# One stacked product for the exponents' row and column terms, and one lane transpose a group, in a hybrid RG-LRU and DeltaNet block

## The chip, the cores and the metric

The kernel runs on one core of one Trainium2 chip. The metric is device time in microseconds (us) of one execution, the median over several. The core has five engines with an instruction queue each: TensorE (PE), which multiplies and whose weight loads are shown apart as PEld; VectorE (DVE); ScalarE (ACT); GpSimd (POOL); and SyncE (SP), which issues the DMAs here.

## What is computed

The reference is a two-layer block over 256 latent and 256 context tokens of width 1024. Layer 0 mixes tokens with a bidirectional RG-LRU, layer 1 with a bidirectional gated DeltaNet of 8 query/key heads and 16 value heads of 128; each layer is followed by a SwiGLU feed-forward. The change lies in the DeltaNet:

```python
def step(s, xs):
    qc, kc, vc, gc, bc = xs
    gc = jnp.cumsum(gc, axis=-1)
    diff = gc[..., :, None] - gc[..., None, :]
    decay = jnp.where(incl, jnp.exp(jnp.where(incl, diff, 0.0)), 0.0)
    kb = kc * bc[..., None]
    m = jnp.where(strict, jnp.einsum('bhid,bhjd->bhij', kb, kc) * decay, 0.0)
    rhs = jnp.concatenate([vc * bc[..., None], kb * jnp.exp(gc)[..., None]], axis=-1)
    sol = lax.linalg.triangular_solve(m, rhs, left_side=True, lower=True, unit_diagonal=True)
    ...
    attn = jnp.where(incl, jnp.einsum('bhid,bhjd->bhij', qc, kc) * decay, 0.0)
    o = (jnp.einsum('bhcd,bhde->bhce', qc * jnp.exp(gc)[..., None], s)
         + jnp.einsum('bhij,bhje->bhie', attn, v_new))
    ...
```

`decay` is an exponential of a difference of cumulated gates: a term of the row plus a term of the column, with a mask. The kernel uses chunks of 128 tokens in place of 64: four chunks `c` (two of context, two of latents), two directions `d`, and 16 value heads in four groups `g` of four.

## The kernel before, in words

The program is written with a recorder. Each engine call is noted with its operands, and `flush` (line 391) lists the noted instructions on five engines with estimated costs, in order of readiness and of a priority: the instruction's place in the program plus a bias of its stage (`TUNE["bias"]`, line 75). The lower number goes first; when an instruction can go on two engines (`R.copy`: ACT or DVE; `R.tt`: DVE or POOL) the planner picks one. Tiles with a tag share a ring of `bufs` buffers and get them in the order of the program; a tile waits until an earlier one of its tag has been read for the last time. PSUM banks of the tag `tr` (two) go to whoever asks. The planned order is what is emitted, so every line of the profile is line 612, where `flush` makes the calls, and groups are told apart by the names of tiles.

The DeltaNet layer (profile 640 to 1120 us) is a string of stages, `PROG` (line 73). A(h) makes key, values and query of a head from `dn_w_in` (products into `ps_mm` of three terms, hi and lo parts in fp32r; convolution `cu` on DVE and ACT; transposes `ps_kt`, `ps_vt`), and writes key and values to DRAM. Z(i) makes the output gate's input. For each group g of four value heads:

- E(g), line 1357: the logarithm `lb` of the row's factor minus or plus the cumulated gate `gc`, split into hi and lo parts (`cb`), transposed (`ps_cb`) to `cT` (64 rows); then for each of 8 pairs of chunk and direction a call of `exponents` (line 1275) and one exponential of 128x512 on ACT into `gn`.
- N(g), line 1389: products of the key with itself (`ps_g`), times `gn` in place on DVE; then the 32x32 diagonal blocks of the 32 matrices of `gn` are laid side by side (`lw`, line 1417: four DVE transposes, each of one block of 32 partitions), inverted in a loop of 60 small DVE instructions, and transposed back to `ld`, `ldt`. `lw`, `ld`, `ldt` and L's `lw1`, `lw2` share the tag `lane`, three buffers.
- L(g), line 1432: the rest of the inverse out of blocks of 32 and 64, many small products (`ps_w`, `ps_z`).
- P(g), line 1528: four calls of `exponents` into `ps_a`, eight exponentials of 128x256 into the two tiles `at` (two buffers), times query-key products `ps_kq`.
- C(g), line 1552: the recurrence over the four chunks with `gn`, `at` and key and values read back from DRAM. `gn` has two buffers, so E(g+2) waits for C(g).

W(0) begins the output product (`ps_wo`). A call of `exponents` sums three products of 512 columns in a bank: the column term (64 rows of `cT` as weights, `pick` as the moving side; or, for the second direction in P, 128 rows of `rT` and `npick`), the row term (`own` as weights, `rows` moving, 128 rows) and the mask (`below` and `identr`, 128 rows). `rows`, `own`, `npick` and `pick` are made once, ahead of all groups, lines 1247 to 1274.

Of the kernel before, what the change touches and what calls it, by code (L numbers as in the profile page):

```python
# [42 lines left out]
def _shuffle(sh, pattern, sizes):  # L43
# [18 lines left out]
    for g, n in zip(lhs, sh.shape, strict=True):  # L62
# [3 lines left out]
        for a in g:  # L66
# [554 lines left out]
def hybrid_block(ctx: ExitStack, tc: tile.TileContext, I, out, dbg=None):  # L621
# [625 lines left out]
    id64 = piece(64)  # L1247
    V.tensor_tensor(id64, ident[:, 0:64], ident[:, 64:128], OP.add)
    npick = dn.tile([128, 64], F32R, name="npick")
    V.tensor_scalar(npick, id64, -1.0, None, OP.mult)  # L1250
    pick = dn.tile([128, 32], F32R, name="pick")
    V.tensor_tensor(pick[0:64], ident[0:64, 0:32], ident[0:64, 32:64], OP.add)
    mod4 = piece(4)
    V.tensor_reduce(out=mod4, in_=ident.rearrange("p (m h) -> p h m", h=4), axis=AX.X, op=OP.add)
    own = {}
    for sign in (1, -1):
        own[sign] = dn.tile([128, 16], F32R, name=f"own{sign + 1}")
        t = piece(16)
        V.tensor_reduce(out=t, in_=id64.rearrange("p (i h) -> p i h", h=4), axis=AX.X, op=OP.add)
        V.tensor_scalar(own[sign], t, float(sign), None, OP.mult)  # L1260
    gch = dn.tile([128, 2, 2, 4, 16], F32R, name="gch")
    for d in range(2):
        R.copy(gch[:, d, 0], gc[:, :, d, :])
        V.tensor_tensor(gch[:, d, 1], gc[:, :, d, :], gch[:, d, 0].bitcast(F32), OP.subtract)
    pt = bank("tr", "ps_gt")
    for d in range(2):
        T.transpose(pt[:, 128 * d:128 * d + 128], gch[:, d].rearrange("p a c h -> p (a c h)").bitcast(F32), ident)
    rT = dn.tile([128, 2, 128], F32R, name="rT")
    R.copy(rT, pt[:, 0:256].rearrange("p (d i) -> p d i", d=2))
    rows = []  # L1270
    for d in range(2):
        rows.append(dn.tile([128, 4, 128], F32R, name=f"rows{d}"))
        V.tensor_tensor(rows[d], rT[:, d].bitcast(F32).rearrange("p (o i) -> p o i", o=1).to_broadcast([128, 4, 128]),
                        mod4.rearrange("p (h o) -> p h o", o=1).to_broadcast([128, 4, 128]), OP.mult)
    def exponents(g, c, d, sign, bound, col, to, name="ps_e"):

        ps = bank("tr", name)
        p4 = ps.rearrange("p (h i) -> p h i", h=4)
        i = 4 * c + g
        lhs, rhs, n = col  # L1280
# [76 lines left out]
    def stage_e(g):  # L1357
# [14 lines left out]
        cb = dn.tile([128, 2, 32], F32R, tag="cb", bufs=2, name="cb")  # L1372
        lf = lb.rearrange("p c d h -> p (c d h)")
        V.tensor_copy(cb[:, 0], lf)
        V.tensor_tensor(cb[:, 1], lf, cb[:, 0].bitcast(F32), OP.subtract)
        pt = bank("tr", "ps_cb")
        T.transpose(pt[0:64, 0:128], cb.rearrange("p a s -> p (a s)").bitcast(F32), ident)
        cT = t["cT"] = dn.tile([128, 128], F32R, tag="cT", bufs=2, name="cT")
        V.tensor_copy(cT[0:64], pt[0:64, 0:128])
        for c in range(4):  # L1380
            for d in range(2):
                s = sidx(c, d, 0)
                p4 = exponents(g, c, d, (1, -1)[d], 1, column(t, c, d), [gn])
                S.activation(gn[:, s:s + 4, :], p4, AF.Exp)

    def column(t, c, d):
        return t["cT"][0:64], pick[0:64, 4 * (2 * c + d):4 * (2 * c + d) + 4], 64

    def stage_n(g):
# [444 lines left out]
```

## Time and profile before

| | us |
|---|---|
| median of 3 runs | 1363.38 |
| lowest and highest | 1362.26, 1370.28 |
| profiled execution | 1364.68 |
| its span | 1363.0 |

The profiled execution is the one that the views below come from. Its granted TensorE clock is 0.976 of full speed on the mean. Of the page's groups of instructions, the one that the change removes from DVE reads 16 transposes of 32x1024 with 32.0 us; the exponents' products keep PE busy for 33.9 us in E (`ps_e`, 96 products) and 16.0 us in P (`ps_a`, 48 products). A row of the windows gives for a stretch how long each engine was busy, with the number of instructions, the granted clock and the DMAs' share. Products are pipelined: the duration of one is longer than its distance to the next, so costs are read from starts. In the chain of waits each piece is a start, a length, and the work or wait that held the end back at that time.

### The profile page before, as it was taken

To read this page: it belongs to the slowest core of one execution; us is meant where nothing else is said; L and a number is where in the kernel's file an instruction comes from. 1 tells how busy PE (TensorE), PEld (TensorE's weight loads), DVE (VectorE), ACT (ScalarE), POOL (GpSimd) and SP (SyncE) were. 2 spreads that over 40 slices of the span, in tenths; PEclk is the share of its full clock that TensorE was granted. 3 is DMA by queue.
4 is the path that set the end of the run, shared out by engine and by line. 5 is a ranking of instruction groups with operands and counts; after the bars stand their busy time and mean duration, and the time that the engine had idled before them with its cause. 6 is when DMAs were issued, how large, how long until landed. Compare 5 with 4: busy or idle time off the path is not lost.

```text
span 1363.0 us, 23260 instructions
## 1 busy us (share of the span) xinstructions
PE 1308.6 (96%) x9200; PEld 1110.3 (81%) x9200; DVE 1035.0 (76%) x1851; ACT 564.9 (41%) x1053; POOL 229.6 (17%) x203
## 2 busy tenths in 40 slices
PE   5999999899999999999998999999998998999997
PEld 3677778878888888888867788898798888999997
DVE  5799986988775665557868889798499376877775
ACT  3388773444321111005746656747646431211100
POOL 2000000110100001212524333334243100000000
PEclk9899999899999999999999999999999699999999
DMA  9545423365564665333523222323133025455563
GB/s 352 197 165 188 140 94 114 124 202 196 188 228 164 192 208 183 98 110 125 178 74 129 71 78 79 105 71 121 63 117 117 25 92 180 139 182 180 179 181 116
DMA packets 61261, 195.60 MB, mean 144 GB/s; under 512 B 6752, under 2 KB 9952, under 8 KB 60896
## 3 DMA queue, kind: packets, MB, share of 16 engines
q1 hardware_dynamic: 61152, 194.12, 42.8%
q8 instruction: 72, 1.18, 0.4%
q14 instruction: 37, 0.30, 0.1%
HBM read 184.13 MB, written 9.96 MB: 142 GB/s over the span
## 4 chain that ended last, share of the span: by engine, by line
PE 56%; issue 15%; DVE 6%; ACT 4%; DMA 1%; POOL 0%; POOLq 0%; SPq 0%; ACTq 0%; DVEq 0%
PE ps_mm L612 29%; PE ps_dn L612 9%; PE ps_e L612 2%; PE ps_wo L612 2%; PE ps_y L612 2%; PE ps_w L612 2%; PE ps_z L612 2%; PE ps_s L612 1%; DVE lw L612 1%; PE ps_ks L612 1%; DVE cu L612 1%; PE ps_a L612 1%; PE ps_qs L612 1%; PE ps_o L612 1%; ACT gn L612 1%
## 5 line engine op out<-in xcount | busy, mean ns | idle before, releaser
L612 PE MATMUL ps_mm<-hh,whi 128*128 128x512 f32 (+1 forms) x888 | 327.4, 370 | 8.0 <-DVE cu L612 5.6
L612 PE MATMUL ps_mm<-hl,whi 128*128 128x512 f32 (+1 forms) x888 | 327.3, 370 | 0.9 <-DVE hl L612 0.8
L612 PE MATMUL ps_mm<-hh,wlo 128*128 128x512 f32 (+1 forms) x888 | 326.2, 368 | 1.7 <-POOL wlo L612 1.7
L612 DVE TENSOR_TENSOR wlo<-raw,whi 128x1024 fp32r<-128x1024 f32 (+2 forms) x183 | 220.5, 1205 | 17.4 <-ACT whi L612 8.3
L612 DVE CAST whi<-raw 128x1024 fp32r<-128x1024 f32 (+2 forms) x177 | 120.2, 679 | 145.8 <-PE ps_mm L612 81.0
L612 POOL TENSOR_TENSOR wlo<-raw,whi 128x1024 fp32r<-128x1024 f32 x55 | 132.0, 2402 | 506.5 <-DVE whi L612 351.3
L612 PEld LDWEIGHTS ps_mm<-hh,whi 128*128 128x128 f32 x888 | 169.6, 191 | 40.6 <-issue 9.9
L612 PEld LDWEIGHTS ps_mm<-hh,wlo 128*128 128x128 f32 x888 | 169.7, 191 | 29.6 <-POOL wlo L612 2.4
L612 PEld LDWEIGHTS ps_mm<-hl,whi 128*128 128x128 f32 x888 | 170.0, 192 | 27.4 <-DVE hl L612 2.0
L612 PE MATMUL ps_dn<-fh,wlo 128*128 128x256 f32 (+1 forms) x374 | 122.7, 328 | 0.0
L612 PE MATMUL ps_dn<-fl,whi 128*128 128x256 f32 (+1 forms) x374 | 122.5, 327 | 0.0
L612 PE MATMUL ps_dn<-fh,whi 128*128 128x256 f32 (+1 forms) x374 | 122.2, 327 | 0.0
L612 PE MATMUL ps_mm<-h2h,whi 128*128 128x256 f32 x352 | 100.4, 286 | 1.1 <-ACT h2h L612 1.1
L612 PE MATMUL ps_mm<-h2l,whi 128*128 128x256 f32 x352 | 100.6, 286 | 0.5 <-DVE h2l L612 0.3
L612 PE MATMUL ps_mm<-h2h,wlo 128*128 128x256 f32 x352 | 100.1, 284 | 0.0
L612 ACT ACTIVATE whi<-raw 128x1024 fp32r<-128x1024 f32 (+2 forms) x61 | 63.2, 1036 | 77.8 <-PE ps_mm L612 45.1
L612 ACT ACTIVATE fh<-sg 128x256 fp32r<-128x256 f32 (+1 forms) x43 | 22.4, 522 | 156.4 <-DVE sg L612 156.3
L612 ACT ACT_TABLE_LOAD x59 | 75.7, 1283 | 7.0 <-DMA sm<-small 3.4
L612 PEld LDWEIGHTS ps_dn<-fl,whi 128*128 128x128 f32 x374 | 71.1, 190 | 6.4 <-issue 0.4
L612 PEld LDWEIGHTS ps_dn<-fh,wlo 128*128 128x128 f32 x374 | 71.1, 190 | 6.4 <-issue 0.4
L612 PEld LDWEIGHTS ps_dn<-fh,whi 128*128 128x128 f32 x374 | 71.1, 190 | 6.0
L612 DVE SCALAR_TENSOR_TENSOR x<-ring,cs,x 128x1024 f32<-128x1024 f32 x49 | 63.9, 1304 | 15.4 <-DMA ring<-ada_w 14.4
(326 smaller groups left out, 2544.7 us busy)
## 6 DMA issues: line engine op xcount, KB each, us to landing
ring<-ada_w SPq DMA_DIRECT2D x96, 512.0 KB, 4.5
raw<-ffn_gu SPq DMA_DIRECT2D x88, 512.0 KB, 3.5
raw<-dn_w_in SPq DMA_DIRECT2D x49, 512.0 KB, 3.5
raw<-ffn_down SPq DMA_DIRECT2D x34, 512.0 KB, 3.6
raw<-rg_w_in SPq DMA_DIRECT2D x16, 512.0 KB, 4.5
raw<-ffn_down SPq DMA_DIRECT2D x17, 384.0 KB, 3.4
raw<-dn_w_out SPq DMA_DIRECT2D x12, 512.0 KB, 3.6
raw<-rg_w_out SPq DMA_DIRECT2D x10, 512.0 KB, 3.4
```

The source lines that it names most:

```text
L612: call(*[real(x) for x in args], **{n: real(v) for n, v in kw.items()})
```

## The change

The row term and the column term become one product of 128 rows. Per group, `src` holds the cumulated gate of the group's four heads in hi and lo parts (64 columns), ones (64), `lb` in hi and lo parts (64), ones (64) and the gate's parts again (64). Three transposes of 128 columns each, starting at parts 0, 1 and 3, put these along the partitions in one bank `ps_src`; `spread` multiplies them on DVE, reading PSUM, with masks of 0, 1 and -1 into `X` (4x128 columns, one copy a head), `Y` (8x128, one a pair of chunk and direction, with the sign) and `Y2` (2x128, for P's second direction). `src`, `X`, `Y` and `Y2` have one buffer each and are used by E and P of the group. `exponents` then has two products: weights from `Y` or `Y2` with `X` moving, and the mask as before. The setup's `pick`, `npick`, `own`, `gch`, `rT`, `rows` and its two transposes go; masks `mod4`, `own`, `own2` are made instead.

In N, ACT copies the four rows of diagonal blocks to one tile `lc` of 128x1024 (tag `lane`), and one DVE transpose makes `lw` from it.

The order of stages changes: P0 goes ahead of E1, C0 behind A4 and A5, P1 ahead of E2 and P2 ahead of E3, Z1 ahead of N3. The bias of L0 to L2 goes from -1500 to -2200 (L3 has its own). `g0` in `TUNE` is read nowhere.

```diff
-PROG = "A0 A1 E0 A2 N0 A3 E1 L0 P0 N1 C0 A4 A5 E2 P1 L1 N2 C1 A6 Z0 A7 E3 L2 P2 N3 Z1 C2 Z2 Z3 L3 W0 P3 C3"
+PROG = "A0 A1 E0 A2 N0 A3 P0 E1 L0 N1 A4 A5 C0 P1 E2 L1 N2 C1 A6 Z0 A7 P2 E3 L2 Z1 N3 C2 Z2 Z3 L3 W0 P3 C3"
...
-    def exponents(g, c, d, sign, bound, col, to, name="ps_e"):
+    def spread(out, part, mask, n):
+        V.tensor_tensor(out, part.rearrange("p (o i) -> p o i", o=1).to_broadcast([128, n, 128]),
+                        mask.rearrange("p (n o) -> p n o", o=1).to_broadcast([128, n, 128]), OP.mult)
+    def exponents(lhs, rhs, bound, to, name):
...
-        T.matmul(p4, lhs, rhs.rearrange("p (h o) -> p h o", o=1).to_broadcast([n, 4, 128]), start=True, stop=False, needs=to)
-        T.matmul(p4, own[sign][:, i:i + 1].to_broadcast([128, 128]), rows[d], start=False, stop=False)
+        T.matmul(p4, lhs, rhs, start=True, stop=False, needs=to)
         lhs, rhs = (identr, below) if bound > 0 else (below, identr)
         T.matmul(p4, lhs, rhs.rearrange("p (o i) -> p o i", o=1).to_broadcast([128, 4, 128]), start=False, stop=True)
...
+        src = dn.tile([128, 5, 64], F32R, tag="src", bufs=1, name="src")
+        mine = gc.rearrange("p c d h -> p (c d) h")[:, :, 4 * g:4 * g + 4]
+        hi, lo = (src[:, 0, 32 * i:32 * i + 32].rearrange("p (x h) -> p x h", h=4) for i in range(2))
+        R.copy(hi, mine)
+        V.tensor_tensor(lo, mine, hi.bitcast(F32), OP.subtract)
+        R.copy(src[:, 4], src[:, 0])
+        for i in (1, 3):
+            G.memset(src[:, i].bitcast(F32), 1.0)
...
-        T.transpose(pt[0:64, 0:128], cb.rearrange("p a s -> p (a s)").bitcast(F32), ident)
-        cT = t["cT"] = dn.tile([128, 128], F32R, tag="cT", bufs=2, name="cT")
-        V.tensor_copy(cT[0:64], pt[0:64, 0:128])
...
+        X = t["X"] = dn.tile([128, 4, 128], F32R, tag="ex", bufs=1, name="ex")
+        Y = t["Y"] = dn.tile([128, 8, 128], F32R, tag="ey", bufs=1, name="ey")
+        Y2 = t["Y2"] = dn.tile([128, 2, 128], F32R, tag="ey2", bufs=1, name="ey2")
+        for k, i in enumerate((0, 1, 3)):
+            T.transpose(pt[:, 128 * k:128 * k + 128], src[:, i:i + 2].rearrange("p a x -> p (a x)").bitcast(F32), ident,
+                        needs=[X, Y, Y2])
+        spread(X, pt[:, 0:128], mod4, 4)
+        spread(Y, pt[:, 128:256], own, 8)
+        spread(Y2, pt[:, 256:384], own2, 2)
...
+        lc = dn.tile([128, 32, 32], F32, tag="lane", bufs=3, name="lc")
         w = dn.tile([128, 32, 32], F32, tag="lane", bufs=3, name="lw")
         for b in range(4):
             r = slice(32 * b, 32 * b + 32)
-            V.transpose(w[r], gn[r, :, 32 * b:32 * b + 32].rearrange("p s f -> p f s"))
+            S.activation(lc[r], gn[r, :, 32 * b:32 * b + 32], AF.Copy)
+        V.transpose(w, lc.rearrange("p s f -> p f s"))
...
-                col = (rT[:, 1], npick[:, 16 * (2 + c) + 4 * g:16 * (2 + c) + 4 * g + 4], 128) if d else column(t, 2 + c, 0)
-                p4 = exponents(g, 2 + c, d, 1, (1, -1)[d], col, t["at"], "ps_a")
+                lhs = t["Y2"][:, c] if d else t["Y"][:, 4 + 2 * c]
+                p4 = exponents(lhs, t["X"], (1, -1)[d], t["at"], "ps_a")
```

More of the change, by code (lines that the diff above doesn't have):

```diff
@@ L70, in _shuffle @@
     return a.reshape([int(np.prod([dims[x] for x in g])) for g in rhs])
-PROG = "A0 A1 E0 A2 N0 A3 E1 L0 P0 N1 C0 A4 A5 E2 P1 L1 N2 C1 A6 Z0 A7 E3 L2 P2 N3 Z1 C2 Z2 Z3 L3 W0 P3 C3"
-TUNE = dict(warm=5000, ev=3000, stay=(300, 0), g0=4, early=(1, 2, 4, 6), eb=0, ea=(0, 1, 1, 1), nwo=2, prog=PROG,
-            bias={'C3': -1500, 'N0': 100, 'N': -700, 'Z3': -1200, 'L': -1500, 'E3': 700, 'W': 10000, 'L3': -800, 'E': -300, 'W0': 10000, 'P': -100, 'E0': -300, 'N3': -700, 'P2': 0, 'C': 400, 'A': 700, 'Z': 700, 'C1': 0})
+PROG = "A0 A1 E0 A2 N0 A3 P0 E1 L0 N1 A4 A5 C0 P1 E2 L1 N2 C1 A6 Z0 A7 P2 E3 L2 Z1 N3 C2 Z2 Z3 L3 W0 P3 C3"
+TUNE = dict(warm=5000, ev=3000, stay=(300, 0), early=(1, 2, 4, 6), eb=0, ea=(0, 1, 1, 1), nwo=2, prog=PROG,
+            bias={'C3': -1500, 'N0': 100, 'N': -700, 'Z3': -1200, 'L': -2200, 'E3': 700, 'W': 10000, 'L3': -800, 'E': -300, 'W0': 10000, 'P': -100, 'E0': -300, 'N3': -700, 'P2': 0, 'C': 400, 'A': 700, 'Z': 700, 'C1': 0})
 class _Tile:
@@ L1246, in hybrid_block @@
     R.copy(identr, ident)
[L1247 to L1253, printed above, removed]
-    V.tensor_reduce(out=mod4, in_=ident.rearrange("p (m h) -> p h m", h=4), axis=AX.X, op=OP.add)
[L1255 to L1274, printed above, removed]
-    def exponents(g, c, d, sign, bound, col, to, name="ps_e"):
[L1277 to L1280, printed above, removed]
-        T.matmul(p4, lhs, rhs.rearrange("p (h o) -> p h o", o=1).to_broadcast([n, 4, 128]), start=True, stop=False, needs=to)
-        T.matmul(p4, own[sign][:, i:i + 1].to_broadcast([128, 128]), rows[d], start=False, stop=False)
+    sel = dn.tile([128, 14], F32, name="rowsel")
@@ new lines, in hybrid_block @@
+    mod4, own, own2 = sel[:, 0:4], sel[:, 4:12], sel[:, 12:14]
+    V.tensor_reduce(out=mod4, in_=ident.rearrange("p (m h) -> p h m", h=4), axis=AX.X, op=OP.add)
+    mod32 = piece(32)
+    V.tensor_reduce(out=mod32, in_=ident.rearrange("p (m h) -> p m h", h=4), axis=AX.X, op=OP.add)
+    V.tensor_reduce(out=own, in_=mod32.rearrange("p (x i) -> p i x", i=8), axis=AX.X, op=OP.add)
+    V.tensor_scalar(own[0:64, 1:8:2], own[0:64, 1:8:2], -1.0, None, OP.mult)
+    V.tensor_scalar(own2, own[:, 5:8:2], -1.0, None, OP.mult)
@@ L1283, in exponents @@
+    def spread(out, part, mask, n):
+        V.tensor_tensor(out, part.rearrange("p (o i) -> p o i", o=1).to_broadcast([128, n, 128]),
+                        mask.rearrange("p (n o) -> p n o", o=1).to_broadcast([128, n, 128]), OP.mult)
+    def exponents(lhs, rhs, bound, to, name):
+        p4 = bank("tr", name).rearrange("p (h i) -> p h i", h=4)
+        T.matmul(p4, lhs, rhs, start=True, stop=False, needs=to)
         lhs, rhs = (identr, below) if bound > 0 else (below, identr)
@@ L1371, in stage_e @@
             V.tensor_tensor(lb[:, :, d], lb[:, :, d], gc[:, :, d, 4 * g:4 * g + 4], (OP.subtract, OP.add)[d])
-        cb = dn.tile([128, 2, 32], F32R, tag="cb", bufs=2, name="cb")
-        lf = lb.rearrange("p c d h -> p (c d h)")
-        V.tensor_copy(cb[:, 0], lf)
-        V.tensor_tensor(cb[:, 1], lf, cb[:, 0].bitcast(F32), OP.subtract)
-        pt = bank("tr", "ps_cb")
-        T.transpose(pt[0:64, 0:128], cb.rearrange("p a s -> p (a s)").bitcast(F32), ident)
-        cT = t["cT"] = dn.tile([128, 128], F32R, tag="cT", bufs=2, name="cT")
-        V.tensor_copy(cT[0:64], pt[0:64, 0:128])
+        src = dn.tile([128, 5, 64], F32R, tag="src", bufs=1, name="src")
[6 more added lines that the diff above has]
+            G.memset(src[:, i].bitcast(F32), 1.0)
+        lf = lb.rearrange("p c d h -> p (c d h)")
+        V.tensor_copy(src[:, 2, 0:32], lf)
+        V.tensor_tensor(src[:, 2, 32:64], lf, src[:, 2, 0:32].bitcast(F32), OP.subtract)
+        pt = bank("tr", "ps_src")
+        X = t["X"] = dn.tile([128, 4, 128], F32R, tag="ex", bufs=1, name="ex")
[7 more added lines that the diff above has]
+        spread(Y2, pt[:, 256:384], own2, 2)
         for c in range(4):
@@ L1382, in stage_e @@
                 s = sidx(c, d, 0)
[L1383 to L1387, printed above, removed]
+                S.activation(gn[:, s:s + 4, :], exponents(Y[:, 2 * c + d], X, 1, [gn], "ps_e"), AF.Exp)
     def stage_n(g):
```

## The prediction, made before the changed kernel was run

> **What bounds the kernel now.** I read the page's busy line first, then the table of windows over the DeltaNet stage (640 to 1120 us, the only stage that the change touches), then the list of PE's waits there.
>
> ```profile
> span 1363.0 us, 23260 instructions
> PE 1308.6 (96%) x9200; PEld 1110.3 (81%) x9200; DVE 1035.0 (76%) x1851; ACT 564.9 (41%) x1053; POOL 229.6 (17%) x203
> ...
> 640.00:1120.00 480.00, 461.39 (x4221) 392.49 (x4219) 380.87 (x912) 287.60 (x610) 163.97 (x134) 0.97 0.28 92
> 700.00:720.00 20.00, 15.16 (x76) 12.47 (x77) 19.64 (x29) 7.38 (x10) 7.74 (x4) 0.96 0.26 87
> 1040.00:1080.00 40.00, 35.07 (x544) 31.93 (x543) 19.81 (x39) 20.72 (x39) 9.36 (x8) 0.70 0.20 67
> ...
> PE ps_mm L612 <- DVE cu L612: 5.6, 3, 3.1
> PE ps_wo L612 <- POOL ol L612: 3.2, 2, 2.2
> ```
>
> In a window's row the columns are length, then busy time of PE, PEld, DVE, ACT, POOL, then clock and DMA. PE is busy 461.39 of 480 us, so the stage is TensorE's, with 18.6 us of idle time; DVE is at 381 of 480 and runs full in places (19.64 of 20 at 700 to 720, where PE loses 4.84 us). At 1040 to 1080 the granted clock falls to 0.70. So a product taken off PE should shorten the stage by what it takes there, as long as DVE and the order keep PE fed.
>
> **The exponents' products.** Each of 48 calls of `exponents` (8 in each of four E stages, 4 in each of four P stages) issues three products of 512 columns. The timeline of PE and of its weight loads for one of E's calls, and pieces of the chain of waits (start, length, what):
>
> ```profile
> 682.65 0.48 PE L612 MATMUL ps_e<-pick,cT 64*128 64x512 f32 x1
> 683.06 0.50 PE L612 MATMUL ps_e<-rows,own 128*128 128x512 f32 x1
> 683.40 0.40 PE L612 MATMUL ps_e<-below,identr 128*128 128x512 f32 x1
> 683.73 0.48 PE L612 MATMUL ps_e<-pick,cT 64*128 64x512 f32 x1
> ...
> 682.65 0.18 PEld L612 LDWEIGHTS ps_e<-pick,cT 64*128 64x128 f32 x1 [0.37 <-issue]
> 683.06 0.18 PEld L612 LDWEIGHTS ps_e<-rows,own 128*128 128x128 f32 x1 [0.23 <-issue]
> 683.17 0.19 PEld L612 LDWEIGHTS ps_e<-below,identr 128*128 128x128 f32 x1
> ...
> 348.75 42.19 PE ps_mm L612 x186
> 681.41 1.08 PE ps_e L612 x3
> 982.50 2.13 PE ps_e L612 x6
> 889.13 0.68 PE ps_a L612 x3
> 1032.95 1.07 PE ps_a L612 x3
> 973.37 0.11 PE ps_cb L612
> ```
>
> One call takes 1.08 us from start to start. A dense product of 512 columns takes 42.19/186 = 0.227 us, so three would take 0.68. The other 0.40 stands around the 64-row product: its weights load only when the product before has streamed (PEld idle 0.37), and so do those of the full-height product behind it (0.23), whereas the load of the full-height `below` begins 0.11 us after the full-height `rows` started, under it. E's 32 calls are 17 such pieces of the chain, first and last shown, 32.7 us in all (some are paired by the planner and cost 0.88). P's eight calls with `pick` are at 1.07, its eight with `npick` (128 rows) at 0.68: 14.0 us together.
>
> The change folds column and row terms into one product of 128 rows, so two full-height products stay. At 0.227 each a call is 0.454: E falls to 14.5 (18.2 less), P to 7.3 (6.7 less). Bounds: at best this; at worst the pair costs as `rows` and `below` do now, 0.34 + 0.33 = 0.67, which leaves 11.3 less from E and 3.3 less from P, 14.6 in all. I take the dense value, since the full-height load above is already seen to run under its predecessor. Three transposes a group replace one and the two of the setup go: 12 against 6, at 0.11 each 0.7 us more. PE's net: 24.9 - 0.7 = 24.2 us less.
>
> The Trainium skill speaks against this in "TensorE: Matmul & The Clock Gate", section "The mechanism": weight loads overlap products in flight only when their row groups differ. By that rule the new pair, equal in rows, would wait both times as the 0.67 above, and the sum would hold 14.6 instead of 24.9. The full-height load at 683.17 under the full-height product of 683.06 disagrees with it here.
>
> **The building of X, Y, Y2 and the lane transposes.** Groups of instructions of this stage (count, busy us, mean ns):
>
> ```profile
> L612 DVE STREAM_TRANSPOSE lw<-gn 32x1024 f32<-32x1024 f32 x16 | 32.0, 2001 | 0.3
> L612 DVE STREAM_TRANSPOSE ld<-lw 128x1024 f32<-128x1024 f32 x4 | 8.2, 2050 | 0.1
> L612 DVE TENSOR_TENSOR rows<-rT,scratch 128x512 fp32r<-128x512 f32 x2 | 1.3, 688 | 0.0
> L612 DVE TENSOR_TENSOR wlo<-raw,whi 128x1024 fp32r<-128x1024 f32 (+1 forms) x16 | 17.4, 1088 | 1.8 <-ACT whi L612 1.3
> L612 DVE TENSOR_TENSOR oa<-ps_o,oa 128x256 f32<-128x256 f32 x32 | 13.0, 418 | 0.5 <-PE ps_o L612 0.3
> L612 ACT ACTIVATE whi<-raw 128x1024 fp32r<-128x1024 f32 x30 | 31.7, 1056 | 36.5 <-PE ps_mm L612 21.6 <-issue 11.8 <-POOL wlo L612 2.4
> L612 ACT ACTIVATE gn<-ld 32x512 f32<-32x512 f32 x15 | 9.4, 626 | 0.5 <-DVE ld L612 0.3
> L612 ACT ACTIVATE gn<-ps_e 128x512 f32<-128x512 f32 x32 | 18.6, 596 | 13.9 <-PE ps_e L612 13.7
> L612 ACT ACTIVATE at<-ps_a 128x256 f32<-128x256 f32 x32 | 10.5, 379 | 9.7 <-PE ps_a L612 9.7
> ```
>
> A 32-partition transpose of 1024 columns costs as much as one of 128 partitions (2.00 and 2.05). So a group's four (8.0 us of DVE) become one of 2.05, behind four ACT copies of 32x1024. These aren't in the trace: twice the 0.63 of 32x512 is 1.25, the 128x1024 copy is 1.06; I take 1.06, 4.2 us a group. `spread` makes 512, 1024 and 256 columns: 0.69 + 1.2 + 0.42 = 2.3 us (the middle one between the 1.09 of a row that mixes in narrower ones and twice 0.69). DVE: 16 transposes out and 4 in, 23.8 us less; spreads 9.2 more; the setup's `rows` 1.4 less; the small copies and splits of 32 to 128 columns, some gone and some new, I set against each other: 16 us less net. ACT: 17 us more on 288 of 480 busy, off the path while it stays the lesser engine; without that cover, a group's copies and one transpose are still 6.3 us against 8.0. POOL's added memsets of 64 columns and the removed constants stand beside PE work at 640 to 680 and count nothing; were they bare, each is under 0.7 us (the 512-column `rows` row). No DMA is added or moved to another queue; the stages that load (A, C, Z, W) keep their order among themselves except that C0 follows A4 and A5, so its `kspill` and `vspill` reads on SP's queue come behind those stages' weights. I give that nothing either way: C0 then has more time, not less.
>
> **The stall that goes.** Behind the first group's transposes (DVE and PE, timeline):
>
> ```profile
> 707.64 2.01 DVE L612 STREAM_TRANSPOSE lw<-gn 32x1024 f32<-32x1024 f32 x1
> 711.89 0.36 PE L612 MATMUL ps_mm<-hh,whi 128*128 128x256 f32 x1 [1.70 <-DVE cu L612]
> 715.28 1.93 DVE L612 STREAM_TRANSPOSE lw<-gn 32x1024 f32<-32x1024 f32 x1
> 718.13 0.47 PE L612 MATMUL ps_mm<-hh,whi 128*128 128x512 f32 x1 [3.13 <-DVE cu L612]
> ```
>
> PE waits 1.70 and 3.13 us for convolutions (`cu`) that stand in DVE's queue between four transposes. Six of their eight us leave DVE. Bounds: 0 (another DVE item in their place, or stage P0's masks, which now come first) to 4.8; I take 3. The 3.2 us for `ol` at 1047 are other work and I leave them.
>
> **Waits that are added.** X, Y, Y2 and `src` have one buffer each, so E of a group waits until P of the one before has read them, and P waits for the `at` tiles, which C of the group before that holds. `lane` has three buffers and one tile more passes through.
>
> ```profile
> 792.16 1.99 DVE L612 STREAM_TRANSPOSE lw<-gn 32x1024 f32<-32x1024 f32 x1
> 795.26 0.22 PE L612 MATMUL ps_z<-gn,lw 64*64 64x64 f32 x1
> ...
> 837.30 0.70 PE L612 MATMUL ps_e<-pick,cT 64*128 64x512 f32 x2
> 838.97 1.72 PE L612 MATMUL ps_o<-yy,at 128*128 128x128 f32 x14
> ```
>
> E2 begins at 837.4 now, before C0's last reads of `at` (to 840.7). Then P1 has 8 exponentials of 0.38 (3.0 us), the three transposes 0.33, and X and Y take 1.9 before E2's first product: about 845.9, 8.5 us later than now. Behind that wait on DVE stand `cu` and `r` of other stages, on PE only the products of this group. E2 itself goes at ACT's 0.60 a call, not at 1.02 (3.4 us back), and N2 wins 1.7: 3.4 us late in sum. N1's transpose needs the slot that `ps_z<-gn,lw` of L0 frees at 795.5, so it ends at 797.6, not 794.2: 3.4 late. Both delays have A products beside them, so I price them 0; bare, they are 6.8 us. E0 starts 1.9 later behind X and Y, under A2's products: 0.
>
> **Sum.** 1364.68 (the profiled execution, span 1363.0) - 24.2 - 3 = 1337.5. That execution is 1.3 us above the median of the runs, 1363.38; I say 1337.
>
> **Rivals.** (a) The groups' chain E, N, L, C sets the length, and PE's saved time turns to idle. For it: DVE at 381 of 480 and the single buffers. Against: 18.6 us idle in the whole stage. Then E2's 3.4 and N1's 3.4 are paid, the stall's 3 comes back, E0, E1, E3 are each shorter by 8 times 0.42 less the 1.9 of the masks: near 1364.7 + 6.8 - 3 - 4.5 = 1364, or 1361 to 1360 if the stall goes whole (1.8 more) with the low clock at and behind it (0.04 of 20 us, twice). That is also the case that the change doesn't do what it says. (b) Slower: E2 behind P1 behind C0 leaves PE dry, as at 1040 to 1080, where the clock is 0.70 and 40 us hold 12 us less clock. With the 6.8 bare, nothing gained and half such a stretch more, 6: 1377. It decides if E2's first product comes more than some 24 us (what PE saves) behind C0's last `ps_o`. Against it: A4 to A7 and Z0 are free to fill. The Trainium skill, "TensorE: Matmul & The Clock Gate", section "What's actually happening", has a clock that halves after an idle window of 3.4 us; the 0.96 row around the stall of 3.13 and the 0.70 row agree. (c) By weight loads that never overlap at equal height, 14.6 - 0.7 + 3 = 16.9 less: 1348. (d) N3, shorter by 6 us of DVE, lets L3 run among dense products and the low clock at 1040 to 1080 goes: 1337 - 12 = 1325.
>
> **How the numbers follow.** Forecast 0.60 (own range 1329 to 1348), (a) 0.18, (b) 0.07, (c) 0.05, (d) 0.10. About 1% of 1363, or 13.6 us, is what a measurement of this kernel tells from no change, so faster means below 1350: forecast, (c) and (d) with a little of them lost, 0.73; slower means above 1377, half of (b) and a little more, 0.05; 0.22 between. The range goes from (d)'s 1325 to 1360, into (a); outside it are (b), half of (a) and the far edge of (d), 0.2.
>
> **What would show it.** Right: `ps_e` in the chain at some 0.46 a call and ACT's exponentials at 0.6 back to back; no DVE transposes of 32x1024, four of 128x1024 more; PE's busy time in the stage near 437; no PE wait for `cu` of over 2 us near N0. Wrong: pairs at 0.67; PE idle in the stage well above 19 us, with `ps_e` or `ps_a` released by DVE `ex`/`ey` or by ACT; a longer stretch of low clock; or DVE above 85% busy with PE waiting for it.

## The result, and the profile after

| | us |
|---|---|
| changed kernel, median of 6 runs (lowest to highest) | 1377.26 (1373.15 to 1381.53) |
| kernel before, on the same chip, median of 6 runs | 1363.59 |
| ratio, 95% interval | 1.0116 (1.0086 to 1.0147) |
| profiled execution of the changed kernel (the lowest of the six), its span | 1373.15, 1371.4 |

The changed kernel is slower by 13.7 us; 1337 was forecast. In the views, the page's head and the clock's line come first; then windows (columns as before); then PE's waits from 640 to 1120.

```profile
span 1371.4 us, 23247 instructions
...
PE 1301.3 (95%) x9158; PEld 1117.0 (81%) x9158; DVE 1032.5 (75%) x1855; ACT 580.1 (42%) x1061; POOL 238.3 (17%) x216
...
PEclk8999999999999999999999999999689699999999
```

```profile
640.00:1120.00 480.00, 442.05 (x4077) 387.72 (x4077) 366.73 (x894) 293.98 (x605) 170.04 (x145) 0.93 0.26 87
700.00:720.00 20.00, 19.73 (x101) 16.09 (x101) 17.95 (x36) 13.96 (x28) 9.66 (x5) 1.00 0.30 106
960.00:980.00 20.00, 13.71 (x274) 12.45 (x274) 16.70 (x27) 14.95 (x24) 9.18 (x9) 0.81 0.40 133
980.00:1000.00 20.00, 18.22 (x239) 17.08 (x232) 0.00 (x0) 8.34 (x19) 0.95 (x1) 0.50 0.01 2
...
PE ps_w L612 <- ACT lw L612: 5.5, 3, 4.1
PE ps_w L612 <- DVE ldt L612: 4.8, 2, 4.0
...
PE ps_mm L612 <- DVE cu L612: 1.5, 2, 1.3
```

PE's busy time in the stage is 442 us; before it was 461 and 437 was forecast. So the work did go. The stall for `cu` went too: 1.5 us are left of 5.6, and 700 to 720 is full. But the clock's mean fell from 0.97 to 0.93, PE now waits in `ps_w` (stage L) for its own copies, and at 980 to 1000 stands something that the profile of before doesn't have: clock 0.50, DVE at 0.00, almost no DMA.

To see where the time went, the DeltaNet stage is cut out of each trace and its length split. It runs from 130 us behind the first product into `ps_dn` of layer 0 to the first product with `h2h`, the feed-forward's input; and it is cut once more where the fourth group's inversion loop begins (the first `lmul` behind the last `memset` of `lw`). In windows of 10 us, "idle" is the length less PE's busy time, "low clock" is busy time times (1 - granted clock), "work" is what is left.

| us | before | after | |
|---|---|---|---|
| length up to the fourth loop | 373.6 | 391.9 | +18.3 |
| idle, low clock | 12.5, 2.5 | 30.3, 19.0 | +34.3 |
| work | 358.6 | 342.6 | -16.0 |
| length behind it | 157.6 | 152.7 | -4.9 |
| idle, low clock | 12.3, 13.5 | 14.8, 10.7 | -0.3 |
| work | 131.8 | 127.2 | -4.6 |

The stage is 13.4 us longer, close to the 13.7 of the medians. The two profiled executions differ by 8.5 only, since the changed kernel's reaches the first `ps_dn` 5.1 us sooner (492.6 and 497.7; in the traces of this document that point lies between 492.6 and 499.7, in kernels of either form). PE does 20.6 us less work in the stage; idle time and low clock take that and more, and all of that lies ahead of the fourth loop.

The pages' chains of the work that ended last, by engine, before and after:

```profile
PE 56%; issue 15%; DVE 6%; ACT 4%; DMA 1%; POOL 0%; POOLq 0%; SPq 0%; ACTq 0%; DVEq 0%
```

```profile
PE 50%; issue 16%; DVE 9%; ACT 8%; DMA 1%; POOL 0%; POOLq 0%; SPq 0%; DVEq 0%; ACTq 0%
```

PE holds less of the chain, DVE and ACT together 17% of it and not 10%. In the stage up to the fourth loop, E's products (`ps_e`) make 32.7 us of the chain before and 3.7 after.

Rows of both kernels show what that loop waited for. First before, then after: PE's and DVE's timelines, and PE's groups within a window (first and last start behind the durations).

```profile
973.21 0.27 PE L612 MATMUL ps_cb<-ident,cb 128*64 128x128 f32 x1
...
985.56 1.95 PE L612 MATMUL ps_g<-kT 128*128 128x128 f32 x16
...
1001.29 0.19 DVE L612 TENSOR_TENSOR lmul<-lw 128x30 f32<-128x30 f32 x1
```

```profile
969.73 0.40 PE L612 MATMUL ps_e<-ex,ey 128*128 128x512 f32 x1
...
970.20 0.28 PE L612 MATMUL ps_mm<-hh,wlo 128*128 128x256 f32 x1
971.22 1.20 PE L612 MATMUL ps_w<-ldt,gn 32*32 32x32 f32 x64 [0.74 <-DVE ldt L612]
976.55 1.76 PE L612 MATMUL ps_w<-ldt,gn 32*32 32x32 f32 x58 [4.14 <-ACT lw L612]
...
998.05 2.07 PE L612 MATMUL ps_g<-kT 128*128 128x128 f32 x8
...
1000.23 2.74 DVE L612 SCALAR_TENSOR_TENSOR gn<-ps_g,gn 128x256 f32<-128x256 f32 x8 [23.03 <-PE ps_g L612]
...
1011.50 1.93 DVE L612 STREAM_TRANSPOSE lw<-lc 128x1024 f32<-128x1024 f32 x1
...
1014.54 0.18 DVE L612 TENSOR_TENSOR lmul<-lw 128x30 f32<-128x30 f32 x1
```

In both kernels the key products of N3 (`ps_g`) release the masks, transposes and loop behind them: 15.7 us from the first `ps_g` to the loop before, 16.5 after. Before, L2 was over by 973 with dense products between its own, then E3 came, then `ps_g`. After, E3 has ended at 970.2, but L2 stands in PE's queue between E3 and N3. From the first of its products (971.22) to `ps_g` (998.05) pass 27 us, some 20 of them after E3's last exponential, which `ps_g` waits for too (it ends at 977.8). PE waits for L2's copies and runs small products at a clock of 0.81 and 0.50, and DVE stands empty for 23 us, since all that it has next is behind `ps_g`. Of the projection products (`ps_mm`) none is left to run beside L2: 1071 have started from 620 to 971, and none to 1005.

```profile
620.00:971.20 351.20, 225.87 (x1071) 172.63 (x1071) 70.53 (x107) 17.89 (x30) 0.97 0.31 105
971.20:1005.00 33.80, 0.00 (x0) 0.00 (x0) 0.00 (x0) 0.00 (x0) 0.60 0.07 24
```

The same cut of the kernel before has 64 of them inside L2:

```profile
620.00:947.80 327.80, 199.44 (x910) 148.35 (x910) 68.20 (x101) 13.53 (x23) 0.99 0.30 102
947.80:973.00 25.20, 9.47 (x64) 7.85 (x63) 4.44 (x7) 1.56 (x3) 1.00 0.29 96
```

In part they were used up earlier, in the E stages: 106 `ps_mm` products start inside the four of them after, 32 before. E itself became hardly shorter. From its first `ps_e` to its last it takes 10.0, 10.3, 9.7 and 8.6 us in the four groups, where it took 11.5, 10.2, 10.3 and 10.2. ACT's timeline in E0 after:

```profile
682.11 1.09 ACT L612 ACTIVATE gn<-ps_e 128x512 f32<-128x512 f32 x2
683.23 1.28 ACT L612 ACT_TABLE_LOAD   x1
684.52 0.63 ACT L612 ACTIVATE kT<-cu 128x512 f32<-128x512 f32 x1
685.17 1.28 ACT L612 ACT_TABLE_LOAD   x1
686.46 1.09 ACT L612 ACTIVATE gn<-ps_e 128x512 f32<-128x512 f32 x2
```

The exponentials stand there between other work of ACT and the loads of tables (1.28 us each) around it. So PE was relieved in E, but what waits for E was not. This is read from the traces; no run tries it.

### The profile page after: what moved, and what is told of

Read it like the earlier page. It is cut to its first block, busy times and chain, and to the rows that moved or that the text cites. A ratio compares the mean times of both kernels' runs of the same rounds, so it can differ in the third digit from the quotient of the medians.

```text
span 1371.4 us, 23247 instructions
## 1 busy us (share of the span) xinstructions
PE 1301.3 (95%) x9158; PEld 1117.0 (81%) x9158; DVE 1032.5 (75%) x1855; ACT 580.1 (42%) x1061; POOL 238.3 (17%) x216
## 4 chain that ended last, share of the span: by engine, by line
PE 50%; issue 16%; DVE 9%; ACT 8%; DMA 1%; POOL 0%; POOLq 0%; SPq 0%; DVEq 0%; ACTq 0%
PE ps_mm L612 26%; PE ps_dn L612 9%; PE ps_y L612 2%; PE ps_wo L612 2%; PE ps_z L612 2%; PE ps_w L612 2%; ACT gn L612 1%; PE ps_s L612 1%; ACT L612 1%; ACT junk L612 1%; PE ps_ks L612 1%; DVE cu L612 1%; DVE gn L612 1%; PE ps_qs L612 1%; DVE lw L612 1%
## 5 line engine op out<-in xcount | busy, mean ns | idle before, releaser
L612 DVE CAST whi<-raw 128x1024 fp32r<-128x1024 f32 (+1 forms) x174 | 118.7, 682 | 160.6 <-PE ps_mm L612 81.1
L612 DVE TENSOR_TENSOR wlo<-raw,whi 128x1024 fp32r<-128x1024 f32 (+2 forms) x180 | 216.7, 1204 | 16.5 <-ACT whi L612 7.7
L612 POOL TENSOR_TENSOR wlo<-raw,whi 128x1024 fp32r<-128x1024 f32 x58 | 139.5, 2407 | 497.3 <-DVE whi L612 364.1
L612 ACT ACTIVATE whi<-raw 128x1024 fp32r<-128x1024 f32 (+2 forms) x64 | 66.0, 1032 | 68.4 <-PE ps_mm L612 39.4
```

What stands on the lines that cost most here:

```text
L612: call(*[real(x) for x in args], **{n: real(v) for n, v in kw.items()})
```

## The experiments

The numbers of theories below are those of the expectations; they were formed one after another, and most fell. Each ratio is to the kernel before, run on the same chip.

### The parts alone

`order_only` is the kernel before with the new `PROG` and L's bias of -2200. `lane_only` is the kernel before with the copies into `lc` and one transpose. `stack_minorder` has the stacked product without the lanes, and of the order only what it needs, each P ahead of the next E; `both_minorder` has both edits with that order; L's bias is as before in both.

```diff
-PROG = "A0 A1 E0 A2 N0 A3 E1 L0 P0 N1 C0 A4 A5 E2 P1 L1 N2 C1 A6 Z0 A7 E3 L2 P2 N3 Z1 C2 Z2 Z3 L3 W0 P3 C3"
+PROG = "A0 A1 E0 A2 N0 A3 P0 E1 L0 N1 C0 A4 A5 P1 E2 L1 N2 C1 A6 Z0 A7 P2 E3 L2 N3 Z1 C2 Z2 Z3 L3 W0 P3 C3"
```

> The kernel before with only the new order of stages and the new bias of L (-2200). Theory 1, the order uses up the products of A ahead of L2, so that L2 and L3 run alone at a low clock: the order alone carries the loss, some 15 us or more over 1363, with a stretch of granted clock near 0.5 around L2. Theory 2, the single buffers of X, Y, Y2 and src tie E to P: nothing of it is in this kernel, 1363 within 5. Theory 3, the copies on ACT and the lane slots: also absent here, 1363 within 5.

> The kernel before with only the ACT copies and the single lane transpose. Theory 1: a gain of 3 to 6 us (some 1358), the wait for cu near 711 to 718 us shrinks. Theory 2: the same. Theory 3: slower by 5 us or more, with L or N waiting for lane slots or for ACT.

> The changed kernel with the four DVE transposes and the bias of L as before, and of the new order only what the single buffers need: each P(g) ahead of E(g+1). Theory 1: most of the 24 us of products shows, 1340 to 1350. Theory 2: no gain or a loss, 1363 to 1378, PE idle around the E stages. Theory 3: as theory 1.

> Both edits, with the bias of L as before and of the new order only each P(g) ahead of E(g+1); C0 stays ahead of A4 and A5, N3 ahead of Z1. Theory 1: 1335 to 1345. Theory 2: near the changed kernel's 1377. Theory 3: slower than the kernel with the stacked products alone by 5 or more.

| | median us | ratio (95%) |
|---|---|---|
| `order_only` | 1383.77 | 1.0162 (1.0099 to 1.0226) |
| `lane_only` | 1374.73 | 1.0078 (1.0049 to 1.0106) |
| `stack_minorder` | 1379.73 | 1.0150 (1.0087 to 1.0214) |
| `both_minorder` | 1372.38 | 1.0072 (1.0043 to 1.0101) |

Each part is slower than the kernel before by itself, and both edits together (1.0072) are no slower than the copies alone (1.0078). The order and L's bias alone, with no instruction added or taken away, cost 21 us. The parts don't add; `flush` lists all instructions anew after any edit. Each of theories 1 to 3 meets some of these times and misses others. Theory 1 has the size of `order_only`, but not its own mark: L2 is covered there (PE busy 27.93 of 28.80 us from 967.7, clock 1.00), and E3 comes behind it.

### What PE's time is worth

Each call's mask product is issued twice, the first time with neither start nor stop, at emission, so that the planned order stays (the mask is then added twice). That is 48 products, by 0.227 us some 11 us of PE.

```diff
         for e, op in order:
...
+            if e == "PE" and kw.get("stop") and not kw.get("start") and "below" in (args[1].t.name, args[2].t.name):
+                call(*[real(x) for x in args], start=False, stop=False)
```

> The kernel before, its order of instructions unchanged on every engine, with the mask product of each of the 48 calls of exponents issued twice (the sum of two masks is the same mask). Each costs 0.227 us of PE. Theory 1, the length is set by PE's work: 48 x 0.227 = 11 us slower, near 1374. Theory 4, the length is set by the chain of loop, L and next loop and by the order on DVE, and PE's time has room: at most 4 us slower.

> The changed kernel with the mask product issued twice in the same way, order otherwise unchanged. Theory 1: 11 us slower than the changed kernel, near 1388. Theory 4: at most 4 us slower, 1377 to 1381.

`before_extra` took 1374.34 beside 1362.32, 12.0 more: in the kernel before, the added work has its full price. That fits PE's time as the bound, but a chain of waits as well: the products stand in E and P, so they delay the groups too, and the four loops begin 2.6, 4.7, 6.6 and 10.0 us later. `after_extra` took 1381.17, 3.9 above the changed kernel's 1377.26, or 5.2 when each is set against the kernel before on its own chip. There half to two thirds of the 11 us are lost, and the stage's idle time falls from 45.1 to 40.5 us. So a price that was measured by adding to PE did not hold for taking away.

### The loop's scratch buffer

The scratch tile `lmul` of the inversion loop shares the tag `xo`, one buffer, with the tile `xo` of stage L. In the traces the second and the third loop begin right behind L's last read of it, in both kernels: PE's group `ps_z<-lw,xo` ends its starts at 801.5 and 888.6 before, 817.4 and 912.0 after. The third loop before and the second after:

```profile
888.85 0.21 DVE L612 TENSOR_TENSOR lmul<-lw 128x30 f32<-128x30 f32 x1 [0.58 <-PE ps_z L612]
```

```profile
L612 PE MATMUL ps_z<-lw,xo x32: 218/218/267, 815.6 to 817.4; 64*64 64x64 f32 x32
...
817.68 0.21 DVE L612 TENSOR_TENSOR lmul<-lw 128x30 f32<-128x30 f32 x1 [0.26 <-PE ps_z L612]
```

By this read loop, L, loop is a chain. The edit gives `lmul` a ring of its own:

```diff
-        m = dn.tile([128, 256], F32, tag="xo", bufs=1, name="lmul")
+        m = tmp(256, name="lmul")
```

> Both edits with the least change of order (as in the run of that kind before, 1372), and the loop's product tile lmul taken from the ring t2k of six buffers instead of sharing the one buffer xo with L, so that the loop of a group need not wait for L of the group before. Theory 4: the link is what binds, the loops of groups 1 and 2 begin earlier and the time falls by 8 to 15 us, near 1360. Theory 5, DVE's total work and not the link: no change, 1370 within 4.

> The kernel before with lmul out of the shared buffer, nothing else. Theory 4: no gain, since E3's products stood behind L2 in that kernel and its last loop began 28 us after L2's end; the new order may cost, 1362 to 1385. Theory 7, the shared buffer alone made the gain and the edits none: 1345 to 1355.

> The changed kernel as given, with its order of stages, and lmul out of the buffer that it shares with L. Theory 4, L2 before the loop of the last group is what the shared buffer holds back: the last loop begins ahead of the end of L2 and the time falls by 8 to 18 us, 1359 to 1369. Theory 6, the gain of the kernel with the least order came from its order alone: 1377 within 4.

> The kernel with the stacked products alone and the least change of order (1380), with lmul out of the shared buffer, so the four lane transposes on DVE as before. Theory 4: the freed buffer gives it what it gave the kernel with both edits, 1360 to 1366. Theory 10, what an edit gives here follows from how the planned order falls out, not from the edit: any time from 1355 to 1385, and PE's work near 470 of the stage all the same.

> The faster kernel (1355) with the mask product of the 48 calls issued twice, order unchanged, 11 us of PE. Theory 4, PE still has room there: at most 5 us slower, 1355 to 1360. Theory 1: 1366.

| | median us | ratio (95%) |
|---|---|---|
| `both_lmul_free` (`both_minorder` and the edit) | 1355.11 | 0.9941 (0.9915 to 0.9966) |
| `before_lmul_free` | 1382.01 | 1.0159 (1.0134 to 1.0184) |
| `after_lmul_free` | 1382.63 | 1.0161 (1.0138 to 1.0185) |
| `stack_lmul_free` | 1376.97 | 1.0114 (1.0066 to 1.0162) |
| `both_lmul_free_extra` (and the doubled masks) | 1362.92 | 1.0008 (0.9991 to 1.0025) |

One complete version beats both kernels: 1355.11, by 17.3 below `both_minorder` and 7.2 below the kernel before. The same edit alone loses 20 us in the kernel before, gains nothing in the order of the change, and gains 2.8 with the stacked products alone, less than the spread of the runs. So the freed buffer is not what made the gain by itself. In `after_lmul_free` the second loop begins at 325.0 from the first `ps_dn`, where it began at 325.1: its lane transpose stands 8 us behind the four copies in both. What `both_lmul_free` does differently stands in its timelines of PE and DVE, and its windows:

```profile
955.29 1.95 PE L612 MATMUL ps_g<-kT 128*128 128x128 f32 x16
967.42 3.62 PE L612 MATMUL ps_w<-ldt,gn 32*32 32x32 f32 x128 [8.74 <-DVE ldt L612]
...
988.75 1.93 DVE L612 STREAM_TRANSPOSE lw<-lc 128x1024 f32<-128x1024 f32 x1 [11.62 <-PE ps_z L612]
...
960.00:980.00 20.00, 11.20 (x353) 10.77 (x354) 11.21 (x25) 13.24 (x23) 3.11 (x3) 0.59 0.16 55
980.00:1000.00 20.00, 19.03 (x136) 17.02 (x134) 10.46 (x32) 6.66 (x11) 1.85 (x3) 0.56 0.00 1
...
L612 DVE TENSOR_TENSOR lmul<-lw x30: 169/344/812, 990.8 to 1025.9; 128x30 f32<-128x30 f32 x2, 128x58 f32<-128x58 f32 x2, 128x84 f32<-128x84 f32 x2, 128x108 f32<-128x108 f32 x2
```

Here L2 is as bare as in the changed kernel: PE idles 8.8 of 20 us, the clock is 0.59 and 0.56. But N3's `ps_g` stands ahead of it, so that N3's masks pass before L2's products, and its copies, its transpose and the beginning of the fourth loop beside them (DVE 11.21 and 10.46, not 0.00). It isn't free of L2: the transpose waits 11.62 us for a product of L2, with which it shares only the ring `lane`, and the loop begins at 990.8, 35.5 us behind `ps_g`. From the first `ps_dn` that is 24.8 us sooner than in the changed kernel all the same. Bare small products at low clock thus stand in the fastest version too; what they hold up is what differs.

`both_lmul_free_extra` is 7.8 above its base: the added work costs about 70% of its length there.

### Four priorities

`both_lmul_free_bias` is `both_lmul_free` with other biases: L -1100, E0 -700, N3 -800, Z 1100 in place of -1500, -300, -700, 700.

> The same with four priorities moved: L -1100, E0 -700, N3 -800, Z 1100. Theory 4, the order of instructions decides the length while PE's work stays as it is: faster than the last by 5 to 12 us, 1345 to 1355, with the same busy time of PE. Theory 1: the same as the last within 4.

It took 1368.06, 1.0025 (0.9997 to 1.0052), 13 us more than without; a miss. Four numbers that change no instruction move the time by as much as the whole change did.

### Half the loop

Of the 30 steps of each inversion loop (two instructions each) the 15 with an even column count are left out at emission, the order unchanged; the inverse is then incomplete.

> The changed kernel with every other step of the inversion loops left out (60 of 120 pairs of lmul and lw, some 10 us of DVE in each of four loops), so the inverses are not computed; the order of all other instructions is unchanged, and PE's work is the same. Theory 1, PE's work sets the length: 1377 within 4. Theory 4, the loops on DVE stand on the path that sets the length: 15 to 40 us faster, 1337 to 1362, with less idle time of PE.

It took 1370.82, 1.0066 (1.0045 to 1.0088), only 6.4 below the changed kernel (4.7 when each is set against the kernel before on its own chip), where 15 to 40 were expected. DVE's work in the loops is the smaller part of what sets their length: with some 10 us of it gone from each, the four loops last 62.8, 58.8, 48.0 and 42.9 us in place of 69.8, 61.1, 54.5 and 45.6. Their steps stand in DVE's queue between other work, such as convolutions that wait for PE. This part of theory 4 falls.

### L2 left out

The products of L2 and the copies that read them are left out at emission, in both kernels, the order unchanged; the inverse of the third group is then only that of its 32x32 blocks.

```diff
+            if op.part == "L2" and any(isinstance(x, _AP) and x.t.psum for x in list(op.args) + list(op.kw.values())):
+                continue
```

> The changed kernel with stage L2's small products and the copies that read them left out, so the third group's inverses are not completed; the order of all other instructions is unchanged. Theory 8, L2 stands alone on PE because the products that could run beside it were used up before it: the time falls by 22 to 34 us, to 1343 to 1355. Theory 9, L2 is covered or its end does not hold the rest: at most 12 us less, 1365 or more.

> The kernel before with the same left out of L2. Theory 8: L2 ran beside products there, so only its own PE time goes, 6 to 13 us less, 1350 to 1357. Theory 9: as much less as in the changed kernel, within 5.

The changed kernel falls by 24.0 us, to 1353.25 (0.9950, 0.9926 to 0.9974), or by 21.7 when each is set against the kernel before on its own chip; the kernel before by 4.6, to 1356.67 beside 1361.31 (0.9955, 0.9930 to 0.9980). So by the medians L2 costs 17 to 19 us more in the changed kernel; by the stages of the four traces, one execution each, it is 12.0 (21.9 and 9.9). That is about the size of the loss. With L2 out of both, the two kernels can't be told apart: the intervals overlap, and the stages end at 652.7 and 651.3. So in these two orders L2's place carries the loss; why some 20 us less work on PE buy nothing it doesn't say. The loop's start says the same: with L2 gone it comes 22.3 us earlier in the changed kernel and 5.4 in the kernel before (times from the first `ps_dn`, in the table below).

### Dense products kept for L2

`after_z1_held`: Z1's 96 projection products wait for `ldt` of the third group, so that L2 has them beside it.

```diff
-            ps = product(I["dn_w_in"][32 + t], NK, hxl, 256)
+            ps = product(I["dn_w_in"][32 + t], NK, hxl, 256, hold=R.mark(X[2][1]) if i in (1,) else ())
```

> The changed kernel with the products of stage Z1 (96 of 256 columns, some 11.5 us) held until the loop of the third group has ended, so that they can run beside L2. Theory 8: low clock and idle time at L2 fall, 5 to 15 us less, 1362 to 1372. Theory 9: no gain, 1377 within 4.

It took 1373.22, 1.0076 (1.0054 to 1.0099), 4.0 below the changed kernel, or 1.8 when each is set against the kernel before on its own chip. The intervals overlap, so no gain is shown, where 5 to 15 us were expected. The trace says why (window and PE's timeline):

```profile
980.00:1000.00 20.00, 20.00 (x319) 18.75 (x318) 10.50 (x18) 13.00 (x24) 3.93 (x3) 1.00 0.24 80
...
996.75 0.48 PE L612 MATMUL ps_e<-ex,ey 128*128 128x512 f32 x1
...
1005.33 1.95 PE L612 MATMUL ps_g<-kT 128*128 128x128 f32 x16
```

The cover is back, PE full and the clock 1.00. But E3 now comes behind L2 (996.75) and N3 behind E3, and from the first `ps_dn` `ps_g` comes at 505.5, as in the changed kernel (505.4). Covered or bare, N3's key products come behind L2, and the fourth loop begins at 520.3, in the changed kernel at 521.9.

### All of L left out

The same as for L2, for L0 to L3; no inverse goes beyond the 32x32 blocks.

> The changed kernel in its own order, with the small products of all four L stages and the copies that read them left out. With L2's alone left out it took 1353.25, which is only 3.4 below the kernel before with the same left out (1356.67), where 24 less PE work was forecast: some 20 us are still open. Theory 8 widened (the products of L0 and L3 stand just as alone on PE as those of L2, with PE idle and the clock low around them): with all of them gone the changed kernel shows most of the 24, 15 to 24 below the kernel before with the same left out. Rival, theory 11 (what is left open lies in waits for DVE's loops and convolutions around the stages E and N and where the A products have run out, which L's products have nothing to do with): the distance stays at 0 to 8.

> The kernel before in its own order, with the small products of all four L stages and the copies that read them left out. Taken to be compared with the same edit of the changed kernel. Theory 8 widened: L0 and L1 have A products beside them here and L3 has little, so it falls from 1356.67 by what L3 costs uncovered, 10 to 20 us, and stays 15 to 24 above the changed kernel with the same left out. Theory 11: it falls as much as the changed kernel does, and stays 0 to 8 above it.

The changed kernel took 1333.44 (0.9794, 0.9756 to 0.9831), the kernel before 1323.12 (0.9727, 0.9698 to 0.9755). Both theories miss, and by the sign: the changed kernel is 10.3 us slower than the kernel before, although by the split its stage has 19.6 us less PE work (420.9 and 440.5); PE idles more (58.0 and 40.5) and loses more to the low clock (21.8 and 11.6). Here the fourth loop begins at the same time in both (489.4 and 488.6 from the first `ps_dn`), and the changed kernel needs 7.3 us more behind it. What lengthens that end isn't settled. What the pair does show: with all of L out of the way, 20 us less work on PE still buys nothing, so L's place is not the whole cause.

### All runs by the start of the fourth loop

Times from the first `ps_dn` product of each trace, one execution each: N3's first `ps_g` (its weight load), the fourth loop's start, the stage's end, and the difference of the last two.

| | `ps_g` | loop | end | behind the loop |
|---|---|---|---|---|
| `both_lmul_free` | 461.1 | 497.1 | 651.0 | 153.9 |
| `before_no_l2` | 482.3 | 498.2 | 651.3 | 153.1 |
| `both_lmul_free_bias` | 460.3 | 498.7 | 664.1 | 165.4 |
| `after_no_l2` | 484.3 | 499.6 | 652.7 | 153.1 |
| before | 487.6 | 503.6 | 661.2 | 157.6 |
| `both_lmul_free_extra` | 470.0 | 505.8 | 661.2 | 155.4 |
| `stack_lmul_free` | 483.9 | 507.6 | 682.1 | 174.5 |
| `after_lmul_free` | 475.0 | 512.1 | 680.5 | 168.4 |
| `before_extra` | 497.6 | 513.6 | 671.8 | 158.2 |
| `both_minorder` | 497.5 | 514.0 | 671.2 | 157.2 |
| `after_half_loop` | 499.8 | 516.2 | 668.0 | 151.8 |
| `lane_only` | 501.8 | 517.9 | 671.1 | 153.2 |
| `stack_minorder` | 502.7 | 519.0 | 678.3 | 159.2 |
| `after_z1_held` | 505.5 | 520.3 | 667.7 | 147.4 |
| `before_lmul_free` | 506.0 | 521.2 | 681.2 | 160.0 |
| after | 505.4 | 521.9 | 674.6 | 152.7 |
| `order_only` | 508.5 | 524.2 | 677.3 | 153.1 |
| `after_extra` | 509.7 | 526.1 | 677.7 | 151.6 |

In 15 of 18 the stage ends 147 to 160 us behind the start of the fourth loop, whatever PE has to do in it (L3, C3 and the rest of the output product follow, in that order). In the three others it ends 165 to 175 us behind it, and their early `ps_g` gains little: there the loop's start is not the whole account.

## Why the prediction was wrong

**What bounds the kernel: failed here.** The step was "a product taken off PE should shorten the stage by what it takes there, as long as DVE and the order keep PE fed". PE at 461 of 480 us looked like the bound, and `before_extra` fits that, though the work added there delays the groups too. But under it lay a chain: E, the loop, L, the next group's loop, through buffers that they share, and at the end N3's key products behind L2. That the two were about as long in the kernel before is what fits these runs; none shows it by itself. With less work on PE the chain stayed: E, at its head, takes 38.5 us in the four groups in place of 42.1. And the new plan made it longer: the fourth loop begins 18.3 us later, and with L2 left out it begins within 1.4 us of the same time in both kernels. This is the premise of rival (a), to which 0.18 was given. Its price, 1364 to 1360, was too low by 13 to 17, since it took the chain as it was, plus 6.8.

**Waits that are added: priced 0, the term of the sum that broke.** The prediction looked at the right places, E2 and N1, and found them covered by A products. E2 was not the trouble. For N1 it named the lane slot that `ps_z<-gn,lw` frees and made that 3.4 us. In ACT's and DVE's timelines and PE's group after:

```profile
803.60 3.19 ACT L612 ACTIVATE lc<-gn 32x1024 f32<-32x1024 f32 x3
...
813.94 2.06 DVE L612 STREAM_TRANSPOSE lw<-lc 128x1024 f32<-128x1024 f32 x1
...
L612 PE MATMUL ps_z<-gn,lw x32: 218/218/267, 808.9 to 813.4; 64*64 64x64 f32 x32
```

The copies are done at 806.8 and the transpose begins at 813.94, 0.3 us behind that product's last: 7.1 us of waiting, not 3.4. The loop behind it would have waited for `xo` until 817.4 as well. With `xo` out of the way (`after_lmul_free`) it begins no sooner, so the wait for the transpose is enough by itself; no run frees the lane slot alone. The second loop begins at 325.1 from the first `ps_dn`, 304.3 before: 20.8 later. The first loop begins 6.7 us sooner than before and ends 12.2 later. In both kernels it stands still on DVE while N1's 16 masks (`gn<-ps_g`) pass; before for 5.4 us, after with convolutions among them for 13.4 (`lmul` at 746.82, the next step at 760.25). But its length isn't what delays the second loop: in `after_half_loop` it ends 6.7 us sooner, and the transpose to `ldt`, for which L0 waits, still ends 2.0 later (296.3 and 294.3), behind convolutions that wait for PE. DVE's timelines, before and after:

```profile
760.87 5.39 DVE L612 SCALAR_TENSOR_TENSOR gn<-ps_g,gn 128x256 f32<-128x256 f32 x16 [0.42 <-PE ps_g L612]
766.18 0.21 DVE L612 TENSOR_TENSOR lmul<-lw 128x58 f32<-128x58 f32 x1
```

```profile
746.82 0.38 DVE L612 TENSOR_TENSOR lmul<-lw 128x220 f32<-128x220 f32 x1
...
751.15 4.05 DVE L612 SCALAR_TENSOR_TENSOR gn<-ps_g,gn 128x256 f32<-128x256 f32 x12
...
760.25 1.22 DVE L612 TENSOR_TENSOR lw<-lw,lmul 128x220 f32<-128x220 f32 x1
```

A cover was claimed for each wait, and what the chain does with a delay that is covered on PE was never asked. Nor was L2, with its place between E3 and N3, looked at. The order of stages was checked for the queues of DMAs and for E, P and C, not for what stands between a group's E and its N on PE. The experiments without L2 put 12 to 19 us there, about the size of the loss.

**The exponents' products: right.** The pair of full-height products runs dense. PE's timeline after, and a piece of the chain of waits:

```profile
735.92 0.40 PE L612 MATMUL ps_e<-ex,ey 128*128 128x512 f32 x1
736.16 0.39 PE L612 MATMUL ps_e<-below,identr 128*128 128x512 f32 x1
736.39 0.40 PE L612 MATMUL ps_e<-ex,ey 128*128 128x512 f32 x1
...
736.09 0.93 PE ps_e L612 x4
```

Two calls in 0.93 us are 0.465 a call; 0.454 was taken. The stage's PE work fell by 20.6 to 22.0 us (windows of 10 and of 20 us), 24.2 were forecast. What E was to gain by it failed: the exponentials don't stand back to back on ACT, and the 3.4 us by which a stage E was to be shorter (8 times 0.42, in rival (a) and for E2) measured 1.5, -0.1, 0.6 and 1.6. Rival (c), in which a full-height load waits for a full-height product, falls: that would be 0.67. So the rule of the Trainium skill, "TensorE: Matmul & The Clock Gate", section "The mechanism", read as the prediction read it, is not what these rows show.

**X, Y, Y2 and the lanes: right.** Groups of instructions of this stage:

```profile
L612 ACT ACTIVATE lc<-gn 32x1024 f32<-32x1024 f32 x16 | 16.9, 1054 | 0.7 <-DVE gn L612 0.5
...
L612 DVE STREAM_TRANSPOSE lw<-lc 128x1024 f32<-128x1024 f32 x4 | 8.1, 2032 | 3.1 <-PE ps_z L612 3.0
L612 DVE TENSOR_TENSOR ey<-ps_src,rowsel 128x1024 fp32r<-128x1024 f32 x4 | 4.9, 1214 | 0.0
L612 DVE TENSOR_TENSOR ex<-ps_src,rowsel 128x512 fp32r<-128x512 f32 x4 | 2.8, 688 | 1.8 <-PE ps_src L612 1.8
```

1.05, 2.03, 1.21 and 0.69 us against 1.06, 2.05, 1.2 and 0.69. DVE's busy time in 640 to 1120 fell by 14 us (380.9 to 366.7; 16 forecast). No run shows that it bought anything; half of the loops' work, some 40 us of DVE, is worth 4.7 to 6.4 us (`after_half_loop`).

**The stall that goes: right.** 4.1 us of the 5.6 went; 3 were taken.

**Rival (b)** had the sign and the size, 1377, and PE dry at low clock, but at E2 behind P1 and C0, with the price from a slower clock. Of its signs one came true: a longer stretch of low clock. `both_lmul_free` and `after_z1_held` show that this stretch goes with the loss and doesn't make it: the one is fastest with it, the other stays slow without it. The reading of the 0.70 row as a clock that falls after idling was half right: ahead of the fall at the stall PE was busy for 0.40 of 3.41 us (715.12 to 718.53), ahead of the fall in the 0.70 row for 2.07 of 3.42 (1049.61 to 1053.03). **Rival (d)** didn't come: the low clock at L3 stayed (0.76 in 1040 to 1080, where it was 0.70).

**What stays open.** Why the end behind the loop grows in three variants, and in the changed kernel without L; what sets E's pace in the changed kernel besides ACT; how much of the late second loop the lane slot makes; and why the plan puts N3 ahead of L2 in some variants and behind it in others: that would lie in the planner's estimated times, which no run shows.

## What to carry to other kernels

An engine that is busy 96% of the time is not yet a bound for work that is taken away: here 11 us more cost 12, and 21 us less bought nothing; a chain of waits of about the same length under it is what fits. So ask whether the work that goes shortens the stage it stands in, or only fills less of it. In a kernel whose order is planned anew after every edit, an edit's gain is that of the new order, and here four priorities moved 13 us; so it pays to follow one late milestone (here the start of the last loop) through all variants rather than the sum of busy times. And a stage of small products with copies between them cost 5 us by the medians where dense products stood among them and the next group's stage E was still to come, and over 20 where the next group's first products stood ready behind them in the queue.

## What the runs showed of the hardware

The granted clock was 0.50 over 20 us in which PE counts as busy for 18.22, 222 of its 239 products of 32x32 or 64x64 (980 to 1000 after). Busy time by the profile is thus no sign of a full clock. With dense products among L2's the clock was 1.00 (980 to 1000 in `after_z1_held`, PE 20.00). The low stretch after began behind 3.42 us in which PE was busy for 0.22 (972.20 to 975.62), and it went on while PE was busy for 2.5 to 3.4 of each 3.4 us with small products.
